# The order of two products in the head of a Strassen pair: the sixth ahead of the second, their tiles requested an entry sooner

## The chip, the cores and the metric

The kernel runs on one core of a Trainium2 chip. The metric is the device time of one execution, in microseconds. Before the change it is 2478.81 us, the median of 3 runs (2478.05 to 2479.55).

## The reference

Two decoder layers on an input of 1 x 256 x 2048 in float32. Cut to what matters here:

```python
for l in range(DEPTH):                                  # DEPTH = 2
    h = rms_norm(x, mix_norm[l])
    proj = h @ w_in[l]                                  # q | k | v | u, v | gate logits
    ...
    branch_a = sliding_window_attention(q, k, v, sinks[l]) @ w_attn_branch[l]
    branch_b = chunked_sgu(...) @ w_sgu_branch[l]
    merged = gates[..., :D_MODEL] * branch_a + gates[..., D_MODEL:] * branch_b
    x = x + merged @ w_out[l]
    h2 = rms_norm(x, ffn_norm[l])
    x = x + (jax.nn.silu(h2 @ w_gate[l]) * (h2 @ w_up[l])) @ w_down[l]
```

Nearly all of the work is dense products of a 256-row activation with a weight matrix (2048 rows in most, D_FF = 5632 columns in `w_gate` and `w_up`).

## The kernel before

**Splitting.** Every weight tile and every activation is split into a high and a low float32r part, and each product of 128 x 128 by 128 x 512 is made of three matmuls: high by high, low weight by high activation, high weight by low activation (`add_product`, L302 to L311). The activation is the stationary side (the weight load, PEld), the weight tile of 512 columns the moving one.

**Entries.** The weights are worked through in one list, `entries`, made ahead (L172 to L182). An entry stands for one weight tile of 256 x 512, `raw`: its DMA, its split and its matmuls. An ordinary entry (tags X, G, U) goes into both halves of the 256 rows: 12 matmuls. Entries of a Strassen product (P1 to P7) go into one half: 6 matmuls.

**Pairs.** Two weight column blocks, `wa` and `wb`, that are multiplied with the same activation form a pair (`pair`, L124). There are 47. For one block of 512 rows of the contraction, a 2 x 2 block product is done by the Winograd form of Strassen's method, with seven products for eight; the remaining rows are done by ordinary entries (G for `wa`, U for `wb`). The four weight tiles of that block are k11, k12 (upper rows of `wa`, `wb`) and k21, k22 (lower rows). They have a buffer of their own each (`bufs=1`), while the other tiles share five `raw` buffers. The head of a pair is the six products P1, P5, P2, P6, P7, P4; P3 stands in the body.

- P1 takes k11 into accumulator a[1].
- P5 takes k12 - k11 (the subtraction overwrites k11) into a[0]. Then ScalarE (ACT) copies a[0] to `kept` (L332) and a[1] to a[0] (L333).
- P2 takes k21 into a[0].
- P6 takes k22 - k11 (overwrites k11) on top of a[1]. Then VectorE (DVE) adds a[1] to what is in `kept` (L335).
- P7 takes k22 - k12 (overwrites k12) on top of a[1], then DVE adds a[1] and `kept` again (L335).
- P4 takes k21 - k11 (overwrites k21) on top of a[1].

P7 and P4 both write a[1], so they wait for the reading of it at L335. In these two the low part of the weights comes first (`low_first`, L309).

**Interleaving.** The head is woven into the last six entries t0 to t5 of the plan before it (four, if that one has only four): t0 P1 t1 P5 t2 t3 P2 P6 t4 P7 t5 P4.

**Streaming.** `Stream.next` (L226) is called once per entry. At entry number `at` it requests the loads of the entries up to at + 6 (L198, on SyncE's queue, SP), the split of entry at + 3 (L221 on ACT makes the high part `whi`, L222 on DVE the low part `wlo`; 4 buffers of each), and the weight subtractions of entry at + 5 (L209 on DVE). Loads wait for their buffer, splits for theirs.

**Order on the engines.** TensorE (PE) runs in the order in which the program is written. The other engines' instructions are ordered by a scheduler when the program is built, and each engine then takes its own in that order.

The changed lines stand in the loop over `plans`:

```python
if n == 6:
    entries += [t[0], h[0], t[1], h[1], t[2], t[3], h[2], h[3], t[4], h[4], t[5], h[5]]
else:
    entries += [h[0], t[0], h[1], t[1], h[2], h[3], t[2], h[4], t[3], h[5]]
```

Here `h` is the head (h[2] is P2, h[3] is P6) and `t` the tail of the plan ahead.

Of the kernel before, what the change touches and what calls it, by code (L numbers as in the profile page):

```python
# [57 lines left out]
def hybrid_trunk(ctx: ExitStack, tc: tile.TileContext, x, mix_norm, w_in, q_norm, k_norm, sinks,  # L58
# [113 lines left out]
    entries = []  # L172
    for p in plans:
        if p.head:
            h, n = p.head, min(6, len(ahead.body))
            t = [entries.pop() for _ in range(n)][::-1]
            if n == 6:
                entries += [t[0], h[0], t[1], h[1], t[2], t[3], h[2], h[3], t[4], h[4], t[5], h[5]]
            else:
                entries += [h[0], t[0], h[1], t[1], h[2], h[3], t[2], h[4], t[3], h[5]]  # L180
        entries += p.body
        ahead = p  # L182

# [819 lines left out]
```

## Time and profile before

| what | value |
|---|---|
| median of 3 runs | 2478.81 us (2478.05 to 2479.55) |
| the profiled execution | 2476.85 us |
| its span, first to last instruction | 2475.1 us |
| DVE busy | 1929.7 us, 78% |
| ACT busy | 1430.2 us, 58% |
| HBM read | 475.27 MB, 193 GB/s over the span |
| pairs (two L335 additions each, 94) | 47 |

How to read it: one execution is profiled. Busy times are shares of the span. Matmuls overlap, and their ends are modelled, so a matmul of 0.39 us busy time may be followed by the next after 0.23 us. In a timeline row the first number is the start in us from the start of the span, the second the duration, and the bracket the idle time of the engine just before it with what ended it. In a row of a group, "x376 | 151.3, 402 | 3.3" reads: count, busy us in all, mean ns of one, idle us before. A name like `acc<-wlo,sh` gives output and inputs; `uh`, `ul` are the high and low part of an activation block, `sh`, `sl` those of a Strassen sum of blocks (P5, P6, P7, P3).

### The profile page before, as it was taken

How to read it: one execution, taken by the hardware profiler on the slowest of the kernel's cores; microseconds unless marked ns; L12 is line 12 of the kernel's file. 1: busy time of each engine (PE TensorE's matmuls, PEld its weight loads, DVE VectorE, ACT ScalarE, POOL GpSimd, SP SyncE). 2: the span in 40 equal slices, each digit the busy share in tenths (PEclk: the TensorE clock that was granted, in tenths of full speed). 3: DMA queues.
4: the chain of work that ended last, by engine and by line, in shares of the span. 5: the costliest groups of instructions: out<-in, count | busy, mean ns of one | idle time of the engine just before them, and what ended most of it. 6: DMA issues, size and time to landing. Idle time of an engine off the chain costs nothing.

```text
span 2475.1 us, 31205 instructions
## 1 busy us (share of the span) xinstructions
PE 2462.7 (99%) x11088; PEld 2027.7 (82%) x11088; DVE 1929.7 (78%) x2261; ACT 1430.2 (58%) x1794; POOL 282.8 (11%) x527
## 2 busy tenths in 40 slices
PE   9999999999999999999999999999999999999999
PEld 7888888888888888888888888888888888888887
DVE  6798676887877787778887986768878777877786
ACT  5566544575655565556655665446655555655564
POOL 3100002221110111001101000121212001110110
PEclk9999999999999999999999999999999999999999
DMA  8655656576656666575747446666657566656654
GB/s 295 205 176 166 213 198 218 181 240 194 214 195 205 211 191 226 174 226 186 229 152 266 153 160 219 214 203 196 227 186 233 183 218 195 215 196 201 216 191 150
DMA packets 275661, 502.54 MB, mean 203 GB/s; under 512 B 26224, under 2 KB 36048, under 8 KB 275504
## 3 DMA queue, kind: packets, MB, share of 16 engines
q1 hardware_dynamic: 259472, 484.25, 59.8%
q0 software_dynamic: 15712, 16.01, 2.2%
q8 instruction: 87, 1.43, 0.2%
q14 instruction: 70, 0.57, 0.1%
q10 hardware_dynamic: 320, 0.27, 0.0%
HBM read 475.27 MB, written 2.10 MB: 193 GB/s over the span
## 4 chain that ended last, share of the span: by engine, by line
PE 93%; DVE 4%; issue 1%; DMA 1%; ACT 1%; SPq 0%; POOL 0%; DVEq 0%; ACTq 0%
PE acc L310 60%; PE acc L311 30%; DVE wlo L222 2%; DMA raw<-in_w_in_dram 1%; PE po L758 1%; DVE raw L209 1%; PE pt L421 1%; ACT whi L221 0%; PE psc L719 0%; PE ppt L748 0%; PE psg L836 0%; DVE ul L412 0%; DVE kept L335 0%; SPq L384 0%; DVE box L379 0%
## 5 line engine op out<-in xcount | busy, mean ns | idle before, releaser
L222 DVE TENSOR_TENSOR wlo<-raw,whi 128x1024 fp32r<-128x1024 f32 (+1 forms) x1039 | 1265.7, 1220 | 494.6 <-ACT whi L221 481.4
L221 ACT ACTIVATE whi<-raw 128x1024 fp32r<-128x1024 f32 (+1 forms) x1039 | 1098.0, 1058 | 924.6 <-PE acc L311 750.7
L310 PE MATMUL acc<-whi,uh 128*128 128x512 f32 x3114 | 1217.2, 391 | 0.4 <-ACT whi L221 0.2
L310 PE MATMUL acc<-wlo,uh 128*128 128x512 f32 x3114 | 1212.7, 389 | 1.5 <-DVE wlo L222 1.4
L311 PE MATMUL acc<-whi,ul 128*128 128x512 f32 x3114 | 1212.3, 389 | 0.0
L310 PEld LDWEIGHTS acc<-wlo,uh 128*128 128x128 f32 x3114 | 584.7, 188 | 124.5 <-DVE wlo L222 3.9
L311 PEld LDWEIGHTS acc<-whi,ul 128*128 128x128 f32 x3114 | 584.4, 188 | 122.6 <-DVE ul L412 0.2
L310 PEld LDWEIGHTS acc<-whi,uh 128*128 128x128 f32 x3114 | 584.6, 188 | 121.3 <-ACT uh L407 0.8
L384 POOL DMA_DIRECT2D tt<-box x480 | 236.0, 498 | 1714.5 <-DVE box L379 949.9
L209 DVE TENSOR_TENSOR raw<-raw,raw 128x1024 f32<-128x1024 f32 x188 | 229.3, 1220 | 1.3
L310 PE MATMUL acc<-wlo,sh 128*128 128x512 f32 x376 | 151.3, 402 | 3.3 <-DVE kept L335 3.3
L310 PE MATMUL acc<-whi,sh 128*128 128x512 f32 x376 | 147.2, 392 | 0.0
L311 PE MATMUL acc<-whi,sl 128*128 128x512 f32 x376 | 146.7, 390 | 0.0
L310 PEld LDWEIGHTS acc<-wlo,sh 128*128 128x128 f32 x376 | 70.5, 188 | 27.6 <-DVE kept L335 14.5
L311 PEld LDWEIGHTS acc<-whi,sl 128*128 128x128 f32 x376 | 70.6, 188 | 15.2
L310 PEld LDWEIGHTS acc<-whi,sh 128*128 128x128 f32 x376 | 70.7, 188 | 13.2
L335 DVE TENSOR_TENSOR kept<-acc,kept 128x512 f32<-128x512 f32 x94 | 64.1, 682 | 0.0
L338 ACT ACTIVATE acc<-kept 128x512 f32<-128x512 f32 x94 | 54.0, 587 | 8.5 <-DVE kept L335 8.3
L853 DVE SCALAR_TENSOR_TENSOR xs<-acc,xs 128x512 f32<-128x512 f32 (+1 forms) x66 | 41.2, 666 | 7.8 <-PE acc L311 7.8
L942 ACT ACTIVATE hid<-acc,rhalf 128x512 f32<-128x512 f32 x44 | 30.4, 690 | 21.0 <-PE acc L311 21.0
L332 ACT ACTIVATE kept<-acc 128x512 f32<-128x512 f32 x47 | 28.1, 597 | 15.0 <-PE acc L311 15.0
L943 DVE SCALAR_TENSOR_TENSOR hid<-hid,acc 128x512 f32<-128x512 f32 x44 | 29.6, 684 | 8.3 <-ACT hid L942 8.3
(135 smaller groups left out, 878.0 us busy)
## 6 DMA issues: line engine op xcount, KB each, us to landing
raw<-in_w_in_dram SPq DMA_DIRECT2D x239, 512.0 KB, 4.6
raw<-in_w_up_dram SPq DMA_DIRECT2D x176, 512.0 KB, 4.7
raw<-in_w_gate_dram SPq DMA_DIRECT2D x176, 512.0 KB, 4.6
raw<-in_w_down_dram SPq DMA_DIRECT2D x176, 512.0 KB, 4.6
raw<-in_w_out_dram SPq DMA_DIRECT2D x64, 512.0 KB, 4.8
raw<-in_w_attn_branch_dram SPq DMA_DIRECT2D x32, 512.0 KB, 5.5
raw<-in_w_sgu_branch_dram SPq DMA_DIRECT2D x32, 512.0 KB, 4.3
tt<-box POOLq DMA_DIRECT2D x480, 32.0 KB, 4.1
```

The lines of the kernel that those rows point to most:

```text
L209: self.last = nc.vector.tensor_tensor(out=self.raws[d], in0=self.raws[x], in1=self.raws[y], op=ALU.subtract)
L221: nc.scalar.activation(hi[:, i, :], raw[:, i, :], AF.Copy)
L222: self.last = nc.vector.tensor_tensor(out=lo[:, i, :], in0=raw[:, i, :], in1=hi[:, i, :].bitcast(F32), op=ALU.subtract)
L310: nc.tensor.matmul(ps, a, part[:, kk, :], start=first and kk + n == 0, stop=False, skip_group_check=True)
L311: nc.tensor.matmul(ps, b, hi[:, kk, :], start=False, stop=kk == 1, skip_group_check=True)
L332: nc.scalar.activation(p.kept[:, 1, :], a[0], AF.Copy)
L335: nc.vector.tensor_tensor(out=p.kept[:, int(tag == "P7"), :], in0=a[1], in1=p.kept[:, 1, :], op=ALU.add)
L338: nc.scalar.activation(ps, p.kept[:, t, :], AF.Copy)
L384: queue.dma_start(dst[j * B:(j + 1) * B, i], box[i * B:(i + 1) * B, j])
L853: nc.vector.scalar_tensor_tensor(out=xs[:, t, sl], in0=sums[t][:, i * w:(i + 1) * w], scalar=scale, in1=xs[:, t, sl], op0=ALU.mult, op1=AL ...
L942: nc.scalar.activation(th, g[t], AF.Tanh, scale=norm.rh[t])
L943: nc.vector.scalar_tensor_tensor(out=th, in0=th, scalar=1.0, in1=g[t], op0=ALU.add, op1=ALU.mult)
```

## The change

P6 comes straight ahead of P2 in the list of entries. The loads of k21 and k22, which belong to P2, are put to the entry ahead of P6, since P6 needs k22. With that the subtraction for P6 and the split of P6 come an entry sooner in the program, the split of P2 an entry later. All other lines are as before, four lines further down (L335 becomes L339).

```diff
             if n == 6:
-                entries += [t[0], h[0], t[1], h[1], t[2], t[3], h[2], h[3], t[4], h[4], t[5], h[5]]
+                order = [t[0], h[0], t[1], h[1], t[2], t[3], h[3], h[2], t[4], h[4], t[5], h[5]]
             else:
-                entries += [h[0], t[0], h[1], t[1], h[2], h[3], t[2], h[4], t[3], h[5]]
+                order = [h[0], t[0], h[1], t[1], h[3], h[2], t[2], h[4], t[3], h[5]]
+            ahead_of = order[order.index(h[3]) - 1]
+            ahead_of["loads"] = ahead_of["loads"] + h[2].pop("loads")
+            h[2]["loads"] = []
+            entries += order
         entries += p.body
         ahead = p
```

## Prediction

> **What bounds the kernel now.** I read the head of the page first (busy times and the chain of waits), then the waits by engine, then the groups of matmuls, and last the timeline of one pair.
>
> ```profile
> span 2475.1 us, 31205 instructions
> PE 2462.7 (99%) x11088; PEld 2027.7 (82%) x11088; DVE 1929.7 (78%) x2261; ACT 1430.2 (58%) x1794; POOL 282.8 (11%) x527
> PEclk9999999999999999999999999999999999999999
> PE 93%; DVE 4%; issue 1%; DMA 1%; ACT 1%; SPq 0%; POOL 0%; DVEq 0%; ACTq 0%
> ```
>
> TensorE (PE) is the bound: 99% busy at full clock, 93% of the chain. The change takes no matmul away, so it can pay only in time that PE loses between matmuls. Idle PE is 2475.1 - 2462.7 = 12.4 us, but a matmul that starts late while an older one is still counted as busy hides more. Who makes PE and its weight loads (PEld) wait:
>
> ```profile
> PE acc L310 <- DVE kept L335: 3.3, 4, 0.9
> PEld acc L310 <- DVE kept L335: 15.0, 42, 1.3
> ```
>
> Columns: total us, times, longest. One wait stands out: a matmul on L310 waits for `kept`, the VectorE (DVE) addition at L335 that reads accumulator a[1] after P6 and again after P7. PE is seen idle 4 times, 3.3 us in all, but weight loads wait 42 times. What the other 38 cost is read from the timeline of one pair (a `hid` pair, some 960 us in). DVE:
>
> ```profile
> 962.98 1.23 DVE L222 TENSOR_TENSOR wlo<-raw,whi 128x1024 fp32r<-128x1024 f32 x1 [1.37 <-ACT whi L221]
> 964.12 1.22 DVE L209 TENSOR_TENSOR raw<-raw,raw 128x1024 f32<-128x1024 f32 x1
> 965.26 1.22 DVE L222 TENSOR_TENSOR wlo<-raw,whi 128x1024 fp32r<-128x1024 f32 x1
> 966.40 0.68 DVE L335 TENSOR_TENSOR kept<-acc,kept 128x512 f32<-128x512 f32 x1
> 967.00 1.21 DVE L222 TENSOR_TENSOR wlo<-raw,whi 128x1024 fp32r<-128x1024 f32 x1
> 968.47 1.23 DVE L222 TENSOR_TENSOR wlo<-raw,whi 128x1024 fp32r<-128x1024 f32 x1 [0.26 <-ACT whi L221]
> 969.62 0.68 DVE L335 TENSOR_TENSOR kept<-acc,kept 128x512 f32<-128x512 f32 x1
> ```
>
> In order: the split of P7's weights, the subtraction for P4's weights, the split of t5 (the tail entry between P7 and P4), `kept` after P6, the split of P4, one more split, `kept` after P7. And PE with PEld in the same stretch:
>
> ```profile
> 963.05 0.39 PE L310 MATMUL acc<-whi,sh 128*128 128x512 f32 x1
> ...
> 964.41 0.39 PE L310 MATMUL acc<-whi,uh 128*128 128x512 f32 x1
> ...
> 966.68 0.19 PEld L311 LDWEIGHTS acc<-whi,ul 128*128 128x128 f32 x1
> 967.13 0.19 PEld L310 LDWEIGHTS acc<-wlo,sh 128*128 128x128 f32 x1 [0.26 <-DVE kept L335]
> ...
> 966.90 0.39 PE L311 MATMUL acc<-whi,ul 128*128 128x512 f32 x1
> 967.13 0.50 PE L310 MATMUL acc<-wlo,sh 128*128 128x512 f32 x1
> 967.47 0.40 PE L310 MATMUL acc<-whi,sh 128*128 128x512 f32 x1
> 967.71 0.39 PE L311 MATMUL acc<-whi,sl 128*128 128x512 f32 x1
> ...
> 971.35 0.39 PE L310 MATMUL acc<-wlo,uh 128*128 128x512 f32 x1
> ```
>
> The pitch of matmuls is 0.227 us: P6's six run from 963.05 to 964.41 (1.36 / 6). P6 is done at 964.41, yet `kept` starts at 966.40, because DVE works in order and has three other instructions in front of it. It ends at 966.40 + 0.68 = 967.08. P7's first weight load was due beside the matmul of 966.90 and starts at 967.13. The steps to the next two matmuls are 0.34 and 0.24 us, so 0.11 + 0.01 over the pitch: some 0.13 us lost, none of it counted as idle.
>
> **What the stall is worth in all.** By heads: 47 pairs, 42 of them with a wait, 4 of these with PE seen idle. The 38 ordinary ones lose 38 x 0.13 = 4.9 us. One of the long ones:
>
> ```profile
> 540.51 1.22 DVE L222 TENSOR_TENSOR wlo<-raw,whi 128x1024 fp32r<-128x1024 f32 x1
> 541.65 0.68 DVE L335 TENSOR_TENSOR kept<-acc,kept 128x512 f32<-128x512 f32 x1
> 541.07 0.39 PE L311 MATMUL acc<-whi,ul 128*128 128x512 f32 x1
> 542.38 0.50 PE L310 MATMUL acc<-wlo,sh 128*128 128x512 f32 x1 [0.92 <-DVE kept L335]
> ```
>
> Here the start is 542.38 - 541.07 - 0.227 = 1.08 us late, and 0.13 follows as above: 1.21, that is 0.29 more than the idle of 0.92. Four of them: 3.3 + 4 x 0.29 = 4.5 us. Together 4.9 + 4.5 = 9.4 us. A second way, from the groups of matmuls:
>
> ```profile
> L311 PE MATMUL acc<-whi,ul 128*128 128x512 f32 x3114 | 1212.3, 389 | 0.0
> L310 PE MATMUL acc<-wlo,sh 128*128 128x512 f32 x376 | 151.3, 402 | 3.3 <-DVE kept L335 3.3
> L310 PE MATMUL acc<-whi,sh 128*128 128x512 f32 x376 | 147.2, 392 | 0.0
> L311 PE MATMUL acc<-whi,sl 128*128 128x512 f32 x376 | 146.7, 390 | 0.0
> ```
>
> At the undisturbed mean, 1212.3 / 3114 = 0.3893 us, 376 matmuls take 146.4 us. The three `sh`/`sl` groups are over that by 4.9 + 0.8 + 0.3 = 6.0 us; with 3.3 idle, 9.3 us. This is the ceiling of what the change can win from this wait.
>
> **The change part by part.**
>
> P6 ahead of P2. The same 47 x 6 matmuls run in both products, on the same operands; PE's work changes by 0. P6 now ends one product, 1.36 us, sooner (963.05 where it was 964.41), and P2 stands between P6 and t4, so P7 starts 1.36 + 2.72 us after P6's end where it was 2.72. `kept` needs only P6. But in the old order DVE was the late one, not P6, so what counts is where `kept` stands in DVE's queue. I compared the built orders: with few exceptions `kept` after P6 now stands straight behind P4's subtraction and ahead of the split of t5. DVE's pitch for such a split is 966.40 - 965.26 = 1.14 us. So `kept` moves from 966.40 to 965.26 and ends at 965.94; P7's weights are due at 966.90, 0.96 us later. The ordinary stall goes whole: -4.9 us. That a timely `kept` leaves no stall is shown by a head where the old order had it one split ahead already:
>
> ```profile
> 584.27 0.68 DVE L335 TENSOR_TENSOR kept<-acc,kept 128x512 f32<-128x512 f32 x1
> 585.34 0.39 PE L311 MATMUL acc<-whi,ul 128*128 128x512 f32 x1
> 585.57 0.39 PE L310 MATMUL acc<-wlo,sh 128*128 128x512 f32 x1
> 585.79 0.39 PE L310 MATMUL acc<-whi,sh 128*128 128x512 f32 x1
> ```
>
> `kept` ends at 584.95, and P7's first steps are 0.23 and 0.22: nothing lost.
>
> The long stalls. In the head at 541 `kept` moves to 540.51 and ends at 541.19, where the weights were due at 541.07: late by about 0.15 instead of 1.3, so about 0.1 of 1.21 stays. The same head in the second layer repeats it. The other two lie in the crowded input stage, where the new order moves small DVE steps too; between half and all of theirs goes. I take 4.5 - 0.2 - 0.6 = 3.7 us.
>
> The split of t5 is now behind `kept`, so later by 0.60 us (967.00 - 966.40): it ends at 967.1, and t5 runs from 968.6 (967.13 + 0.13 + 1.36). Cover 1.5 us, cost 0; without the cover 47 x 0.6 = 28 us at most. The split of P4 and the second `kept` keep their places in time, since the same work stands ahead of them.
>
> P6's own weights. Their subtraction now stands one split sooner in DVE's queue, and the split of t3 behind it. In the pair shown:
>
> ```profile
> 954.65 1.22 DVE L209 TENSOR_TENSOR raw<-raw,raw 128x1024 f32<-128x1024 f32 x1
> 956.99 2.35 DVE L222 TENSOR_TENSOR wlo<-raw,whi 128x1024 fp32r<-128x1024 f32 x2
> 961.69 0.39 PE L310 MATMUL acc<-whi,uh 128*128 128x512 f32 x1
> ```
>
> The subtraction moves from 954.65 to some 953.5; the first of the two splits at 956.99 is P2's now and P6's then, ready by 958.2, 3.5 us ahead of PE at 961.69. P2's is ready 1.1 us after that and used at 963.05. Cost 0. If a crowded stage used up the 3.5 us, each us more would cost one in that head.
>
> The loads. k21 and k22 go with the entry ahead of P6. SyncE's queue holds the same 896 transfers; by the built orders 5 stand elsewhere. It runs far ahead anyway: k22 of the pair shown is the first row here, the second is the typical time to landing.
>
> ```profile
> 933.59 0.37 SPq L198 DMA_DIRECT2D raw<-in_w_down_dram  x1
> raw<-in_w_down_dram SPq DMA_DIRECT2D x176, 512.0 KB, 4.6
> ```
>
> It lands at some 938.2, 16 us before its first use at 954.65. The loads cost and bring 0; nothing behind them in that queue moves, and POOL's queue is the same.
>
> Sum: -4.9 - 3.7 = -8.6 us. The profiled execution took 2476.85 us, 1.75 us around its span of 2475.1; it becomes 2468.25. It is 1.96 us under the median of 2478.81, so for the median I forecast 2478.81 - 8.6 = **2470.2 us**.
>
> **A rule that speaks against it.** The rows above put the late weight load at 0.23 us and the loss at 0.13. The Trainium skill, page "TensorE: Matmul & The Clock Gate", section "Architectural detail: the array is 16× 32×32, not 1× 128×128", says that PE's queue can pull weight loads ahead of matmuls in flight, while ACT and DVE are strictly first in, first out. By the first half a late weight load would vanish under running matmuls, and only visible idle could be won; the trace agrees in part, as about half of the 0.23 is hidden. The second half agrees with `kept` waiting at 966.40 behind a split that has nothing to do with it.
>
> **The rivals.**
>
> Only the visible idle returns. If the longer steps in P7 (0.34 and 0.24) belong to a load that waits on a semaphore at all, not to lateness, just the 3.3 us of idle go: 2478.81 - 3.3 = 2475.5. For it: the three groups' excess is a modelled busy time. Against it: the head at 585, where the same load has the same wait and no long step. The rule of the page would give this time too. Chance 0.10.
>
> The wait moves from P7 to P4. P4 also waits for a `kept`, the one after P7: 969.62 + 0.68 = 970.30, against a load due at 971.12 - 0.13 = 971.0. Its room is 0.7 us. In the new queue three splits stand between the two `kept` instead of two. If the third made the second `kept` late by a full 1.14 us in each head, P4 would lose 0.44 x 47 = 21 us against 8.6 won: 2478.81 + 12 = 2491. It decides from 0.7 us on, and the forecast turns into a loss from 0.7 + 8.6 / 47 = 0.9. For it: DVE works without a gap from 962.98 to 968.2. Against: the moved split only changes sides, and the last split waits for ScalarE (0.26 at 968.47), which leaves DVE room. Chance 0.06.
>
> Partly so: the crowded input stages lose what their heads gain, because DVE steps there change places (a split late by one pitch of 1.14 us in four heads costs 4.6): 2478.81 - 8.6 + 4.6 = 2474.8. For it: the two long stalls of that stage show DVE behind there. Against: its work is the same. Chance 0.10.
>
> **How the numbers follow.** Forecast 0.74, with its own range 2468.5 to 2472.5: below, the ceiling of 9.4 and 0.9 more from waits that go with it; above, the long stalls only half won (2.3) and the rest of the interval for scatter of the median (0.75 each way by the runs). Visible idle 0.10, crowded stages 0.10, P4 0.06. To leave out no more than 2 in 10 the range runs from 2467.5 to 2475.5. What a measurement can tell from no change is about 0.2%, 5.0 us: faster means under 2473.85. That holds for the forecast and for the better part of the crowded case: 0.74 + 0.05 = 0.79. Visible idle and the rest of the crowded case are no change: 0.15. Slower: 0.06.
>
> **What would show it.** After the change the wait of weight loads on `kept` should fall from 42 times to a handful, and the group `wlo,sh` from a mean of 402 to about 390 ns with its 3.3 us of idle near 0.3. In the timeline of the pair `kept` should start some 1.1 us earlier against P7, which takes its first step in 0.23 us. Idle PE falls only from 12.4 to about 9 us, as most of the gain was never idle. The forecast is wrong if `wlo,uh` of P4 or t5 shows a new wait on `kept` L339 or the split L226, if `whi,sh` of P6 waits for its split, or if the `wlo,sh` mean stays at 402 while `kept` is early.

## The result, and the profile after

| kernel | median | runs | ratio to before, 95% interval |
|---|---|---|---|
| before | 2479.82 us | 11 (2478.05 to 2481.61) | |
| changed | 2473.29 us | 11 (2472.08 to 2474.80) | 0.9975 [0.9967, 0.9983] |

The change gains 6.5 us, 0.25%; the interval is 4 to 8 us. The profiled execution went from 2476.85 to 2473.06 us, its span from 2475.1 to 2471.1. That is 2.5 us less than the medians say. Two traces of one order can lie 1.9 us apart, as the first experiment below shows, and the runs scatter with the granted clock that they list: the 21 runs of before beside that experiment have a median of 2478.57 us at 1.0, 2480.24 at 0.999 and 2481.29 at 0.998, and the 5 runs of the changed kernel at 1.0 have 2473.26, 5.3 us under the first.

The page of the changed kernel, to be read beside the one of before: the busy times, and the groups of matmuls in products with a Strassen sum.

```profile
span 2471.1 us, 31179 instructions
PE 2456.6 (99%) x11088; PEld 2032.1 (82%) x11088; DVE 1925.3 (78%) x2261; ACT 1430.8 (58%) x1794; POOL 283.2 (11%) x527
...
L315 PE MATMUL acc<-whi,ul 128*128 128x512 f32 x3114 | 1213.5, 390 | 0.0
L314 PE MATMUL acc<-whi,sh 128*128 128x512 f32 x376 | 147.3, 392 | 0.0
L314 PE MATMUL acc<-wlo,sh 128*128 128x512 f32 x376 | 147.1, 391 | 0.0
L315 PE MATMUL acc<-whi,sl 128*128 128x512 f32 x376 | 146.5, 390 | 0.0
```

`wlo,sh` fell from a mean of 402 ns with 3.3 us of idle before it to 391 ns with none. By the sum of the prediction: 376 matmuls at 1213.5 / 3114 = 0.3897 us are 146.5 us, the three groups are over it by 0.8 + 0.6 + 0 = 1.4 us, where they were over by 9.3 with the idle. So 7.9 us of the 9.3 went.

But look at idle PE: 2471.1 - 2456.6 = 14.5 us, where it was 12.4. Busy PE fell by 6.1 us with the same 11088 matmuls, idle PE rose by 2.1. Most of the stall that was won had been counted as busy; what was lost shows as idle. Who makes PE and the weight loads wait now:

```profile
PE pt L425 <- DVE gate L928: 2.9, 2, 1.4
PE acc L314 <- DVE wlo L226: 2.2, 5, 0.6
PE ppt L752 <- DVE wsT L623: 2.1, 1, 2.1
PE acc L314 <- ACT uh L411: 1.2, 1, 1.2
...
PE psc L723 <- DVE att L766: 0.7, 1, 0.7
...
PEld acc L314 <- DVE kept L339: 0.7, 3, 0.2
```

The weight loads that waited for `kept` 42 times, 15.0 us, wait 3 times, 0.7 us: twice in P7 of the first pair of an `ffn` stage, and once in a P4, where the kernel before waits as well. In their place stand two waits that the kernel before hardly had: the transposes of `gate` (L425) for the addition at L928, 2.9 us in 2 places (0.2 before), and the scores `psc` for `att`, 0.7 us (none before).

The same `hid` pair as in the prediction, DVE and then PE, after the change:

```profile
961.31 1.23 DVE L226 TENSOR_TENSOR wlo<-raw,whi 128x1024 fp32r<-128x1024 f32 x1 [1.46 <-ACT whi L225]
962.46 1.22 DVE L213 TENSOR_TENSOR raw<-raw,raw 128x1024 f32<-128x1024 f32 x1
963.59 0.68 DVE L339 TENSOR_TENSOR kept<-acc,kept 128x512 f32<-128x512 f32 x1
964.19 2.35 DVE L226 TENSOR_TENSOR wlo<-raw,whi 128x1024 fp32r<-128x1024 f32 x2
966.80 1.22 DVE L226 TENSOR_TENSOR wlo<-raw,whi 128x1024 fp32r<-128x1024 f32 x1 [0.26 <-ACT whi L225]
...
965.24 0.39 PE L315 MATMUL acc<-whi,ul 128*128 128x512 f32 x1
965.46 0.39 PE L314 MATMUL acc<-wlo,sh 128*128 128x512 f32 x1
965.69 0.39 PE L314 MATMUL acc<-whi,sh 128*128 128x512 f32 x1
965.91 0.39 PE L315 MATMUL acc<-whi,sl 128*128 128x512 f32 x1
```

`kept` stands straight behind P4's subtraction (the row ahead of it), ends at 963.59 + 0.68 = 964.27, and P7's first load is due at 965.24. The first step of P7 is 0.23 us where it was 0.34.

**Where time was given back.** DVE around the last gate block of the first layer, first before the change:

```profile
460.49 1.27 DVE L922 SCALAR_TENSOR_TENSOR gate<-gate,acc 128x512 f32<-128x512 f32 x2
461.69 1.22 DVE L222 TENSOR_TENSOR wlo<-raw,whi 128x1024 fp32r<-128x1024 f32 x1
462.82 1.28 DVE L924 TENSOR_TENSOR gate<-gate,gate 128x512 f32<-128x512 f32 x2
464.03 2.35 DVE L222 TENSOR_TENSOR wlo<-raw,whi 128x1024 fp32r<-128x1024 f32 x2
```

and after, with the PE transposes of that block in the last two rows:

```profile
460.72 0.68 DVE L926 SCALAR_TENSOR_TENSOR gate<-gate,acc 128x512 f32<-128x512 f32 x1
461.32 0.68 DVE L928 TENSOR_TENSOR gate<-gate,gate 128x512 f32<-128x512 f32 x1
461.92 2.35 DVE L226 TENSOR_TENSOR wlo<-raw,whi 128x1024 fp32r<-128x1024 f32 x2
464.19 0.68 DVE L928 TENSOR_TENSOR gate<-gate,gate 128x512 f32<-128x512 f32 x1
...
463.21 0.27 PE L425 MATMUL pt<-ident,gate 128*128 128x128 f32 x1
464.93 0.98 PE L425 MATMUL pt<-ident,gate 128*128 128x128 f32 x7 [1.45 <-DVE gate L928]
```

The second addition has slid behind two splits (2.35 us), and PE waits for it. In the second layer the same. Between its neighbours the transpose block takes 1.3 us longer than before, twice, 2.6 us in all. The third place is in the second layer's attention, DVE and PE after the change:

```profile
1416.73 1.22 DVE L213 TENSOR_TENSOR raw<-raw,raw 128x1024 f32<-128x1024 f32 x1
1417.87 0.69 DVE L824 TENSOR_TENSOR v<-v,ln 128x512 f32<-128x512 f32 x1
1418.47 0.42 DVE L766 TENSOR_TENSOR att<-po,rd 128x256 f32<-128x256 f32 x1
...
1417.52 0.71 PE L723 MATMUL psc<-kT,qT 64*128 64x128 f32 x4
1418.94 0.71 PE L723 MATMUL psc<-kT,qT 64*128 64x128 f32 x4 [0.71 <-DVE att L766]
```

The first row is P6's subtraction, an entry sooner than before. It puts `att` back by its pitch of 1.14 us, and the last four of the eight scores matmuls wait for `att`; before, all eight ran in 0.99 us from 1420.31, now they take 1418.94 + 0.71 - 1417.52 = 2.13, so 1.1 us more.

### The profile page after: what moved, and what is told of

It reads as the page before. It is cut to its first block, busy times and chain, and to the rows that moved or that the text cites. A ratio compares the mean times of both kernels' runs of the same rounds, so it can differ in the third digit from the quotient of the medians.

```text
span 2471.1 us, 31179 instructions
## 1 busy us (share of the span) xinstructions
PE 2456.6 (99%) x11088; PEld 2032.1 (82%) x11088; DVE 1925.3 (78%) x2261; ACT 1430.8 (58%) x1794; POOL 283.2 (11%) x527
## 4 chain that ended last, share of the span: by engine, by line
PE 94%; DVE 2%; DMA 1%; SPq 1%; issue 1%; ACT 0%; POOL 0%; DVEq 0%; ACTq 0%
PE acc L314 61%; PE acc L315 30%; DMA raw<-in_w_in_dram 1%; SPq L388 1%; DVE wlo L226 1%; PE po L762 1%; PE pt L425 1%; PE ppt L752 0%; PE psc L723 0%; ACT whi L225 0%; PE psg L840 0%; DVE box L383 0%; POOL rq L286 0%; DVE raw L213 0%; DVE gate L928 0%
## 5 line engine op out<-in xcount | busy, mean ns | idle before, releaser
L315 PE MATMUL acc<-whi,ul 128*128 128x512 f32 x3114 | 1213.5, 390 | 0.0
L315 PE MATMUL acc<-whi,sl 128*128 128x512 f32 x376 | 146.5, 390 | 0.0
L339 DVE TENSOR_TENSOR kept<-acc,kept 128x512 f32<-128x512 f32 x94 | 64.2, 684 | 0.0
L342 ACT ACTIVATE acc<-kept 128x512 f32<-128x512 f32 x94 | 55.1, 587 | 10.8 <-DVE kept L339 10.7
```

The costliest lines, as they stand in the source:

```text
L315: nc.tensor.matmul(ps, b, hi[:, kk, :], start=False, stop=kk == 1, skip_group_check=True)
L339: nc.vector.tensor_tensor(out=p.kept[:, int(tag == "P7"), :], in0=a[1], in1=p.kept[:, 1, :], op=ALU.add)
L342: nc.scalar.activation(ps, p.kept[:, t, :], AF.Copy)
```

## The experiments

Theory A: what pays is the place of `kept` after P6 in VectorE's queue. Theory B: what pays is that P6 itself ends 1.36 us sooner. Theory C: what pays is that k21 and k22 are loaded sooner.

**The loads alone.** The products stand in the old order; the loads of k21 and k22 go with the entry ahead of P2. The edit, against the changed kernel:

```diff
-                order = [t[0], h[0], t[1], h[1], t[2], t[3], h[3], h[2], t[4], h[4], t[5], h[5]]
+                order = [t[0], h[0], t[1], h[1], t[2], t[3], h[2], h[3], t[4], h[4], t[5], h[5]]
...
-            ahead_of = order[order.index(h[3]) - 1]
+            ahead_of = order[order.index(h[2]) - 1]
```

> Products in the old order, only the loads of k21 and k22 an entry sooner. The built program has the same order of instructions on every engine as the kernel before. Theory A (the gain comes from where `kept` after P6 stands in VectorE's queue) and theory B (the gain comes from P6 itself ending 1.36 us sooner) both expect the time of before within 1 us, with the weight loads of P7 waiting 42 times on `kept` as before. Theory C (the sooner loads are what pays) expects most of the 6.5 us gained. Apart from that the run shows how much one trace differs from the next.

Measured: 2478.93 us against 2479.97 of before, ratio 0.9997 [0.9988, 1.0006]. The loads have another place in the program, but the built order is that of before on every engine and on SyncE's queue. So no load went sooner, and the run shows only that the moved loads do nothing by themselves; that they aren't needed either is shown by the next run. Since the order is that of before, the trace says how far two traces differ: a span of 2477.0 against 2475.1, of which the wait on `wsT` has

```profile
PE acc L314 <- DVE kept L339: 3.2, 4, 0.9
PE ppt L752 <- DVE wsT L623: 2.2, 1, 2.2
PE acc L314 <- ACT uh L411: 1.3, 1, 1.3
...
PEld acc L314 <- DVE kept L339: 15.0, 42, 1.3
```

2.2 where the trace of before has 1.6. The wait on `uh` at the start is 1.3 where it has 0.2, but that is soon made up: before has waits of its own at 12 to 16 us, and the same matmul starts at 16.54 us there and at 16.55 here. So these two rows of the changed kernel (2.1 and 1.2) are no effect of the change, and only the one on `wsT`, 0.5 us more than before, makes its span longer.

**The queue alone.** The products and loads stand as before; the split requested at P6, which is that of t5, is held back and queued behind `kept`.

```diff
-        def next(self):
+        def next(self, late=False):
             self.load(self.at + W_LOAD)
-            self.split(self.at + (W_FIRST if self.at < N_FIRST else W_SPLIT))
+            if not late:
+                self.split(self.at + (W_FIRST if self.at < N_FIRST else W_SPLIT))
...
-        w = stream.next()
+        w = stream.next(tag == "P6")
...
-            nc.vector.tensor_tensor(out=p.kept[:, int(tag == "P7"), :], in0=a[1], in1=p.kept[:, 1, :], op=ALU.add)
+            k = nc.vector.tensor_tensor(out=p.kept[:, int(tag == "P7"), :], in0=a[1], in1=p.kept[:, 1, :], op=ALU.add)
+            if tag == "P6":
+                with tc.issue_after(k.ins):
+                    stream.split(stream.at - 1 + W_SPLIT)
```

> Products and loads in the old order, P2 ahead of P6; only the split of t5 is queued behind `kept` after P6 on VectorE. Theory A: P7's waits on `kept` go as in the changed kernel (matmul steps lose 9.4 us less), and as the built order puts the second gate addition of each layer behind two splits here too, 2.6 us come back: 6 to 7 us faster than before. Theory B: P6 ends no sooner, so `kept` is no sooner either: within 1 us of before, wlo,sh at a mean of 402 ns.

Measured: 2471.12 us against 2479.97, ratio 0.9967 [0.9955, 0.9980], 8.9 us, 5 to 11 by the interval, where theory A expected 6 to 7 (the spans are 6.0 apart). It has no product exchanged and is as fast as the changed kernel or faster. Its groups and waits:

```profile
L311 PE MATMUL acc<-wlo,sh 128*128 128x512 f32 x376 | 146.9, 391 | 0.0
...
PE pt L425 <- DVE gate L928: 2.9, 2, 1.4
...
PEld acc L311 <- DVE kept L336: 0.8, 4, 0.2
```

P7's wait is gone just as in the changed kernel, and the gate transposes wait the same 2.9 us, though the edit names no gate instruction: the scheduler moved the addition once `kept` stood elsewhere. The scores do not wait for `att` here, since P6's subtraction is where it was. Theories B and C fall: P6 ends no sooner, the loads are asked for where they were, and the gain is there.

**The changed kernel with `kept` late.** P6 stands ahead of P2; `kept` after P6 is written down at P2 and queued behind the split of t5. (The edit binds the second `kept` to the split ahead of it too; in the pair shown that one stands where it stood.)

```diff
-        elif tag in ("P6", "P7"):
-            nc.vector.tensor_tensor(out=p.kept[:, int(tag == "P7"), :], in0=a[1], in1=p.kept[:, 1, :], op=ALU.add)
+        elif tag in ("P2", "P7"):
+            with tc.issue_after(stream.last.ins):
+                nc.vector.tensor_tensor(out=p.kept[:, int(tag == "P7"), :], in0=a[1], in1=p.kept[:, 1, :], op=ALU.add)
```

> The changed kernel, P6 ahead of P2 and loads sooner, but `kept` after P6 is queued behind the split of t5 on VectorE, where it stood before. Theory A: P7 waits again, 38 x 0.13 + some 4 = about 9 us more than the changed kernel, so 2 to 4 us slower than before, since the 4 to 5 us lost at the gate additions and in the attention stage stay; wlo,sh back at some 402 ns. Theory B: as fast as the changed kernel, about 6.5 us under before, as P6 still ends 1.36 us sooner.

Measured: 2483.97 us against 2479.97, ratio 1.0015 [1.0006, 1.0024], 4.0 us slower than before and some 10 slower than the changed kernel.

```profile
PE acc L314 <- DVE kept L340: 4.8, 7, 0.9
PE psc L724 <- DVE att L767: 0.7, 1, 0.7
PE pt L426 <- DVE gate L929: 0.2, 1, 0.2
...
PEld acc L314 <- DVE kept L340: 17.6, 44, 1.3
...
L314 PE MATMUL acc<-wlo,sh 128*128 128x512 f32 x376 | 151.9, 404 | 4.8 <-DVE kept L340 4.8
```

With P6 just as soon and `kept` behind one split again, the whole wait is back and more: all 44 waits of weight loads on `kept` stand at P7, where before had 40 (its other two are at P4), and PE is seen idle 7 times, not 4. The steps in P7, added up as in the next section, lose 3.0 us more than before. The expectation had the loss at the gate staying; it went (0.2), as the scheduler's order fell the old way there. The wait for `att` stayed, 1.1 us. So the 4.0 us lie in the expected range, but are 3.0 + 1.1 and not the sum that was expected.

**The gate additions first.** The changed kernel, with the split requested by the last entry of each layer's fourth `w_sgu_branch` product queued behind the gate additions (`next` as in the queue-alone kernel).

```diff
+        if p.key[0] == "mix" and ahead.key[0] == "sgu":
+            for e in ahead.body[-1:]:
+                e["late"] = True
...
-        w = stream.next()
+        w = stream.next(e.get("late", False))
...
-                nc.vector.tensor_tensor(out=ga[:, t, :], in0=ga[:, t, :], in1=gb[:, t, :], op=ALU.add)
+                g_ = nc.vector.tensor_tensor(out=ga[:, t, :], in0=ga[:, t, :], in1=gb[:, t, :], op=ALU.add)
+            if j == NCH - 1:
+                with tc.issue_after(g_.ins):
+                    stream.split(stream.at - 1 + W_SPLIT)
```

> The changed kernel, with the split requested by the last entry of each layer's fourth w_sgu_branch product queued behind the gate additions on VectorE. Theory of the give-back: the transposes of the last gate block waited 1.3 us in each layer because a gate addition had slid behind two splits; both waits go, 2.6 us under the changed kernel, so about 9 us under before. Rival: the held split then stalls the next ordinary product by as much, and the time stays that of the changed kernel.

Measured: 2469.88 us against 2479.97, ratio 0.9961 [0.9949, 0.9974]: 10.1 us under before, where the changed kernel is 6.5 under. The wait of the gate transposes is gone from the list of waits. VectorE's order differs from the changed kernel's in six places, three around the gate additions of each layer.

**P6's subtraction an entry later.** The changed kernel, with the subtraction listed at P2 and not at P6.

```diff
-                dict(tag="P2", loads=[l21, l22], src=k21),
-                dict(tag="P6", loads=[], sums=[(k11, k22, k11)], src=k11),
+                dict(tag="P2", loads=[l21, l22], sums=[(k11, k22, k11)], src=k21),
+                dict(tag="P6", loads=[], src=k11),
```

> The changed kernel with the subtraction for P6's weights an entry later, where it stood before the change (P6 still ahead of P2). Theory of the give-back: in the second layer's attention the scores' first matmuls waited about 1.1 us because that subtraction had moved ahead of the `att` multiplication on VectorE; that wait goes. The built order also has only one split, not two, ahead of the second gate addition, so a good part of the 2.6 us there should go as well: 1 to 3.5 us under the changed kernel. Rival: P6's weights are then late and P6 waits for its split, so that the time is that of the changed kernel or above.

Measured: 2474.08 us against 2480.9, ratio 0.9974 [0.9964, 0.9984]; the changed kernel on the same chip has 2474.72, so there is no difference. Half of the expectation held: the wait for `att` is gone. The other half did not.

```profile
PE pt L425 <- DVE gate L928: 2.8, 2, 1.4
...
450.28 0.39 PE L315 MATMUL acc<-whi,ul 128*128 128x512 f32 x1
450.67 0.50 PE L314 MATMUL acc<-whi,sh 128*128 128x512 f32 x1
451.01 0.40 PE L314 MATMUL acc<-wlo,sh 128*128 128x512 f32 x1
...
450.67 0.19 PEld L314 LDWEIGHTS acc<-whi,sh 128*128 128x128 f32 x1 [0.43 <-ACT acc L337]
...
450.04 0.58 ACT L337 ACTIVATE acc<-acc 128x512 f32<-128x512 f32 x1
```

One split ahead of the second gate addition costs as much as two. And in the head ahead of the last gate block P6 loses 0.3 us (steps of 0.39 and 0.34), in each layer, so that the time is that of the changed kernel, as the rival had it. But P6 doesn't wait for its split: it waits for ScalarE's copy of a[1] (L337), which now ends at 450.62, where in the changed kernel it ended at 449.13, ahead of P6 at 449.61.

**Both repairs.** The two edits above together.

> The changed kernel with both repairs: the split behind the gate additions, and P6's subtraction an entry later. If the two places hold all that was given back, 3.7 us under the changed kernel, some 9 to 10 us under before. Rival: another wait takes their place, and it is no faster than either repair alone.

Measured: 2470.08 us against 2480.9, ratio 0.9955 [0.9942, 0.9969], 4.6 us under the changed kernel on the same chip (2474.72), where 3.7 were expected. The two places hold what was given back, nearly all of it at the gates: P6's 0.3 us in each layer are lost here too (449.17 to 449.56), and the two layers' 0.5 us take back about half of the 1.1 us that `att` brings.

**The two queue positions without the exchange.** The queue-alone kernel with the gate additions first.

> The products in the old order, with two queue positions alone: the split of t5 behind `kept` after P6, and the split behind the gate additions. Theory A, by which the order of the products matters only through VectorE's queue, expects the full 9.4 us of P7's waits and nothing given back: 9 to 11 us under before, so at least as fast as any kernel with the products exchanged. Theory B expects it no better than before by more than 2 to 3 us.

Measured: 2468.62 us against 2480.9, ratio 0.9951 [0.9939, 0.9964]: 12.3 us under before (9 to 15 by the interval), the lowest median of all and above the 9 to 11 that theory A expected; the spans are 9.3 apart. The head of its page:

```profile
span 2465.8 us, 31217 instructions
PE 2455.0 (100%) x11088; PEld 2030.5 (82%) x11088; DVE 1927.3 (78%) x2261; ACT 1430.3 (58%) x1794; POOL 279.4 (11%) x527
```

Idle PE is 2465.8 - 2455.0 = 10.8 us, 3.7 less than in the changed kernel.

**The changed kernel again.**

> The changed kernel once more, unaltered, beside the three repairs on the same chip: 6 to 7 us under before by every theory, with the gate transposes waiting 2 x 1.3 us and the scores 1.1 us in the trace again if these come from the built order, and elsewhere if they were chance.

Measured: 2474.72 us against 2480.9, ratio 0.9975 [0.9965, 0.9985], the first result once more.

```profile
PE pt L425 <- DVE gate L928: 2.9, 2, 1.4
...
PE psc L723 <- DVE att L766: 0.7, 1, 0.7
```

Both waits are there again to the tenth; they belong to the built order, which is the same.

## Why the prediction was right, and where not

The forecast was 2470.2 us, 8.6 less; measured were 6.5 less (4 to 8 by the interval). The direction, the place and the mechanism held; the time lies in the stated range, and 0.8 us above the forecast's own range of 2468.5 to 2472.5. Of the 3.1 us between forecast and time 2.1 are gain that didn't come; 1.0 is the median of before, 2478.81 by 3 runs and 2479.82 by 11.

**The stall hidden in busy time.** That the ordinary waits and four long ones make 9.4 us was right. The count was a little off: 40 of the 42 waits stand at P7, the other two (0.18 and 0.24 us) at P4's first load, so there are 36 ordinary ones, 35 that lose 0.13 to 0.14 us and one that loses 0.19. Added up over the traces, the steps between the matmuls of P7, as far as they exceed the pitch of 0.2266 us, come to 9.9 us before and 0.7 after, so 9.2 went (groups of matmuls: 9.3 to 1.4). Putting `kept` back behind one split brought all of it back, and 3.0 us more.

**The 4.9 for the ordinary heads and 3.7 for the long ones.** Both a little low, 5.0 and 4.3 by the trace: the ordinary waits went whole, and of the long ones only 0.1 us stayed in each first pair of the `ffn` stage, as worked out; in the input stage nothing stayed where I had left 0.6.

**"P6 ahead of P2" as the cause.** The working went through DVE's queue and not P6's end, and the runs bear that out more strictly than it said: with no product exchanged, the queue position alone gains 8.9 us; with the products exchanged and the old queue position, 4.0 us are lost.

**The loads at 0.** Right: moved alone they leave the built order as it was (0.9997), and with the loads where they were the queue alone gains 8.9 us.

**The second half of the sum failed.** The term that was mis-sized is what the rest of DVE's order costs, which I put at 0 outside the heads: "The split of P4 and the second `kept` keep their places in time", and the subtraction for P6 at "Cost 0". In the heads both held. But the built order moved a gate addition behind two splits, 2 x 1.3 us, and P6's subtraction put `att` back, 1.1 us: 3.7 us given back, 9.2 - 3.7 = 5.5 by the traces, 6.5 by the medians, 5.3 by the runs at a listed clock of 1.0. I had read the built order only around `kept`. The rival "the crowded input stages lose what their heads gain" had the right kind of loss, 4.6 us of it at the price of one DVE pitch a place, but the main place was the gate additions ahead of `w_out`, which it didn't name.

**The other rivals.** Visible idle alone: refuted, as 6.1 us of busy PE went and idle rose. P4 as the new waiter: refuted; the second `kept` kept its room, and the one wait of P4 that is left (0.24 us) is there before as well. Neither P4 nor t5 waits for its split: the five waits on `wlo` (four before) all lie ahead of the first pair. Of what the changed profile would show, idle PE "to about 9 us" was wrong: it is 14.5, for the losses above and for the waits at the start and on `wsT`, which differ from trace to trace.

## What to carry to other kernels

When an engine is counted as 99% busy, look at the steps between its instructions: here a loss of 0.13 us, 36 times over, stood in no idle column. An instruction that another engine waits for should be queued explicitly ahead of work that has slack; reordering the products paid only by what it did to that queue, and along with it an unrelated addition slid behind splits in each layer and P6's subtraction came ahead of `att`, which took back 3.7 of 9.2 us. Where a scheduler orders the queues, compare the whole built order of the busiest helper engine, not just the part around the change.

## What was not expected of the hardware

What a late weight load costs is its wait less a fixed 0.11 to 0.13 us, in all 40 waits at P7 before the change: a wait of 0.26 us costs 0.13 to 0.14, one of 0.32 costs 0.19, one of 1.06 costs 0.94 and those of 1.34 cost 1.21 and 1.23 (the steps of P7 over the pitch, added up). After the change the two that are left wait 0.21 and cost 0.08 to 0.09. So a fixed amount is hidden and not a share; 0.04 us of it is the ordinary gap between two loads (0.227 - 0.188). That about half of the 0.23 us is hidden, as the prediction has it, holds for the ordinary wait alone.

And two executions of one program differ. The two traces of the changed kernel have spans of 2471.1 and 2473.3 us, and the second falls behind at the start: the matmul that starts at 18.09 us in the first starts at 20.82 in it. Its wait on `uh` at 16.45 us is 1.42 us long, and from 17.3 us on the granted clock is 0.50 for 3.4 us (1.00 in the first trace), with matmuls of 0.63 us in place of 0.39. A single span is some 2 us uncertain for that.
